# A decoder block on one Trainium2 core: the linear attention's norm weight loaded as 128 written-out rows

## The chip, the cores and the metric

The program runs on one core of one Trainium2 chip. A core has five engines with a queue of instructions each: TensorE (PE, with weight loads shown as PEld), VectorE (DVE), ScalarE (ACT), GpSimd (POOL) and SyncE (SP). SP and POOL issue the DMA transfers of this kernel; 16 DMA engines carry them. The metric is the device time in microseconds, the median of several runs.

## The reference, cut to what matters

One decoder layer on a sequence of 2048 tokens of width 1024: a modulation from a condition vector, a norm, one input projection whose columns go to a gated linear attention (4 heads of 128 values) and to a dilated softmax attention, an output projection, and then a convolution feed-forward network. All in float32. The part that the change touches is the linear attention's output: each head's 128 values are normalised, multiplied by a weight `norm_g` of 128 numbers, the same for all 4 heads, and by a gate.

```python
def rms_norm(x, g):
    xf = x.astype(jnp.float32)
    y = xf * lax.rsqrt(jnp.mean(xf * xf, axis=-1, keepdims=True) + EPS)
    return (y * g.astype(jnp.float32)).astype(x.dtype)
...
    o = o.transpose(1, 0, 3, 2, 4).reshape(B, S, H, GLA_DV)     # H = 4, GLA_DV = 128
    o = rms_norm(o, norm_g).reshape(B, S, H * GLA_DV)
    return (o * jax.nn.silu(r.astype(jnp.float32))).astype(r.dtype)
```

## The kernel before

The tokens are cut into four chunks of 512 (T); every tile has 128 partitions (P) of 512 columns. A matrix product in float32 precision is done as three products of rounded parts: each weight block is loaded into `wraw` (2 buffers), split by ACT into `whi` (L240) and by DVE into `wlo` (L241), each with 4 buffers, and `mm3` issues hi times hi, hi times lo, lo times hi (L306 to L308) into a PSUM tile `psg` (4 buffers). So a weight block passes DMA, ACT, DVE and PE in turn.

`run` first computes the modulation and the first norm. Meanwhile it multiplies the first four weight blocks of the input projection (the tuple FIRST, blocks g0 to g3) with the normalised input tile by tile; their four results stand in all four `psg` buffers. Then it calls `consts`, whose loads wait (through `after`) for one of the last instructions of the modulation. Next comes the projection of chunk 0 in the order of ORDER0: "g0 g1 g2 g3" copy the four results out of PSUM (L523, on ACT, into stage tiles that POOL stores), "V0" is a product with 272 columns (24 matmuls for each of four PSUM tiles, named `psg_516`, `psg_543`, `psg_581` and `psg_608` below), and "W1" is the output gate, where the norm weight comes in (L552). Beside it `stats` loads the tokens of chunk 1 (L1119, tile `sq`, 3 buffers, issued by POOL), squares them on ACT (L426) and adds the squares on DVE (L429, L431).

A scheduler that works with a simulated timeline sets the order of the instructions on each engine, so a changed transfer can also move instructions that the source leaves alone. Engines run their queues in order: an ACT instruction that waits holds all behind it.

The lines that the change touches load and use the norm weight; the weight is a row of 128 numbers in memory, and the tile `gB` holds it four times side by side in every partition:

Of the kernel before, what the change touches and what calls it, by code (L numbers as in the profile page):

```python
# [10 lines left out]
F32 = mybir.dt.float32  # L11
# [3 lines left out]
ALU = mybir.AluOpType  # L15
# [4 lines left out]
P = 128  # L20
# [68 lines left out]
def scale_table():  # L89

    h = 2 * np.arange(4)[None, :] + np.arange(P)[:, None] // 64
    return 0.125 * 2.0 ** (h + 1.0)
# [42 lines left out]
class K:  # L135
# [49 lines left out]
    def consts(self):  # L185
        nc, A = self.nc, self.A
        self.ct = self.const.tile(list(CONSTS.shape), F32, name="consts_sb")
        self.after(nc.sync.dma_start(self.ct, A["consts"]))
        n0 = len(self.loads)
        self.mk = self.cload("masks", MASKS.shape, U32)  # L190
        self.halo = self.const.tile([P, 44, 2], F32, name="halo")

        raw = self.at.tile([P, T], F32, name="graw", tag="pt", bufs=5)
        self.gw = self.const.tile([96, 256], F32R, name="gw")
        self.tie(nc.vector.memset(raw[0:96, 0:256], 0.0), self.lastmm)
        for r in (0, 32, 64):
            self.loads.append(nc.sync.dma_start(raw[r:r + 16, 0:256], A["gla_w_gate"]))
            if r < 64:
                self.loads.append(nc.sync.dma_start(raw[r + 16:r + 17, 0:256], A["gla_b_gate"]))
        nc.vector.tensor_copy(self.gw, raw[0:96, 0:256])  # L200
        nc.vector.tensor_tensor(self.gw[32:64], raw[32:64, 0:256], self.gw[32:64].bitcast(F32), op=ALU.subtract)
        self.gB = self.const.tile([P, 4, P], F32, name="gB")
        g = A["gla_norm_g"]
        self.loads.append(nc.sync.dma_start(self.gB, bass.AP(tensor=g.tensor, offset=g.offset, ap=[[0, P], [0, 4], [1, P]])))
        for ld in self.loads[n0:]:
            self.after(ld)
        self.blk = self.const.tile([P, P], F32R, name="blk")

        self.tie(nc.vector.tensor_copy(self.blk, self.C("blk")), self.lastmm)
        self.tri = self.const.tile([P, P], F32R, name="tri")  # L210
        self.tie(nc.vector.tensor_copy(self.tri, self.C("tri")), self.lastmm)
        self.st = self.const.tile([P, 4, P], F32, name="state")
        nc.vector.memset(self.st, 0.0)
        self.sb = []
        for i in range(2):
            t = self.const.tile([P, 4, P], F32, name=f"sbd{i}")
            nc.vector.memset(t, 0.0)
            self.sb.append(t)
# [254 lines left out]
    def proj(self, c, hs, hook=None, done=()):  # L473
        nc, A, D = self.nc, self.A, self.D[c]
# [3 lines left out]
        def stage(tag=None):  # L478
            if tag:
                return self.up.tile([P, T], F32, name="stg", tag=tag)  # L480
            return self.xp.tile([P, T], F32, name="stg", tag="x")
# [47 lines left out]
        def wide(b):  # L529

            pss = [self.pg() for _ in range(4)]
            for j in range(4):
                w = self.weights("w_tokw", b, j)
                order = [(i, s) for i in range(2) for s in range(4)]
                if j == 3:

                    order.sort(key=lambda x: x[1])
                for i, s in order:
                    h, l = hs[2 * j + i]
                    tk = slice(s * P, (s + 1) * P)  # L540
                    self.mm3(pss[s], [(h[:, tk], l[:, tk])], w[i:i + 1], i == 0 and j == 0, True)
                if j < 3:
                    yield
            for s in range(4):
                off = b and put_off
                st = stage("y0" if off else None)
                if b:
                    r = stage("y1" if off else None)
                    nc.scalar.activation(st, pss[s], AF.Tanh, scale=0.5)
                    nc.scalar.copy(r, pss[s])  # L550
                    nc.vector.scalar_tensor_tensor(st, st, 1.0, r, op0=ALU.add, op1=ALU.mult)
                    nc.vector.scalar_tensor_tensor(st, st, 0.5, self.gB.rearrange("p a b -> p (a b)"), op0=ALU.mult, op1=ALU.mult)  # L552
                else:
                    nc.scalar.copy(st, pss[s])
                self.dq.dma_start(D["rg" if b else "gv"][s * P:(s + 1) * P, :], st)
            if b == 1 and hook:
                hook()
            yield
# [35 lines left out]
        def stores(g):  # L594

            for i, _ in enumerate(g):
                if late and i == 0:
                    next(late.pop(), None)
                yield

        ops = dict(W=wide, V=av, g=glaqk, q=qk)
        order = ORDER if c else ORDER0
        if put_off:
            order = order[:-1]
            self.tail = wide(1)
# [559 lines left out]
def pack_blocks(w, cols):  # L1165

    Kk, N = w.shape
    return w.reshape(Kk // P, P, N // cols, cols).transpose(2, 1, 0, 3).reshape(N // cols, P, (Kk // P) * cols)


def pack_down(w):
    out = []
    for g in range(6):
        n = 4 if g < 5 else 2
        out.append(pack_blocks(w[g * 512:g * 512 + n * P], 1024 // n))
    return np.concatenate(out)


def pack_tok(x):

    return x.T.reshape(KD, P, NCH, T).transpose(2, 0, 1, 3)


def colv(v):
    return v.reshape(-1, P).T


def layout(x, c, w_ada, b_ada, norm1_g, w_in, gla_w_gate, gla_b_gate, gla_norm_g, q_norm_g, k_norm_g, w_out, norm2_g, w_up, conv_w, conv_b, w_down):
    w = w_in[0]
    wide = lambda a: a.reshape(4, 2, P, T).transpose(0, 2, 1, 3).reshape(4, P, 2 * T)  # L1190
    half = lambda a, n: pack_blocks(a, n).reshape(-1, P, 2, 4 * n).transpose(0, 2, 1, 3)
    twice = lambda a: np.concatenate([a, a])[:, None]
    tabs = np.concatenate([colv(norm1_g[0]), colv(norm2_g[0]), colv(b_ada[0]), twice(q_norm_g[0]), twice(k_norm_g[0]), conv_w[0].reshape(3, 44, P).transpose(2, 0, 1).reshape(P, 132), colv(conv_b[0]), scale_table()], 1).astype(np.float32)
    arrs = dict(
        consts=CONSTS, masks=MASKS,
        xT=pack_tok(x[0]), c=c[0], tables=tabs,
        w_ada=w_ada[0].T.reshape(48, P, 1024),
       
        w_av0=half(np.concatenate([w[:, 2576:2832], w[:, 1536:1552]], 1), 272)[0],
        w_av1=half(w[:, 2832:3088], 256)[0],  # L1200
        w_tokw=np.stack([wide(w[:, 512:1024]), wide(w[:, 1024:1536])]),
        w_ch=pack_blocks(np.concatenate([w[:, 0:512], w[:, 1552:2576]], 1), P),
        gla_w_gate=gla_w_gate[0], gla_b_gate=gla_b_gate, gla_norm_g=gla_norm_g,
        w_out=pack_blocks(w_out[0], P), w_up=pack_blocks(w_up[0], P), w_down=pack_down(w_down[0]),
    )
    return {n: np.ascontiguousarray(a) for n, a in arrs.items()}
# [16 lines left out]
```

## Time and profile before

| | |
|---|---|
| median of 3 runs | 2603.27 us (2602.47 to 2603.3) |
| span of the profiled execution | 2603.1 us |
| instructions | 46834 |
| busy: PE, PEld | 98%, 81% |
| busy: DVE, ACT, POOL | 74%, 49%, 17% |
| DMA moved, mean rate | 405.13 MB, 156 GB/s |

The profile is one execution; the runs were timed apart. Times in its rows are microseconds from the start of the span. A row of the timeline reads: start, duration, engine, line, operation, what it writes and reads, its shape, how many in a row, and in brackets how long its engine stood idle before it and what ended that. In a row of a table of waits stand the waiting instruction, what it waited for, the sum, the number and the longest. A row of a stretch reads: the stretch, its length, the busy time of PE, PEld, DVE, ACT and POOL with the number of instructions, the granted clock of TensorE as a share of full speed, the mean busy share of the 16 DMA engines, and GB/s.

### The profile page before, as it was taken

What the parts mean: (1) busy time and instruction counts of PE and PEld (TensorE: products, weight loads), DVE (VectorE), ACT (ScalarE), POOL (GpSimd) and SP (SyncE); (2) the same over time, 40 slices, a digit from 0 to 9 for tenths busy, and PEclk for the clock granted to TensorE, in tenths of its full rate; (3) what the DMA queues carried; (4) which work ended last, traced back from release to release, by engine and by line L of the source; (5) the groups of instructions that cost most, each with busy time, mean ns of one, the idle gap of its engine ahead of it and who ended that gap; (6) DMA issues with size and microseconds to landing.
All of it is one profiled execution on the core that took longest, in us unless ns stands there. A gap on an engine that the chain in (4) does not pass through costs nothing.

```text
span 2603.1 us, 46834 instructions
## 1 busy us (share of the span) xinstructions
PE 2559.7 (98%) x18142; PEld 2104.0 (81%) x18142; DVE 1930.2 (74%) x4091; ACT 1277.7 (49%) x2626; POOL 444.4 (17%) x816
## 2 busy tenths in 40 slices
PE   5999999999999999999999999999999999999999
PEld 4888888788788888887788888878888888788887
DVE  7578877768788777777987777689777775766665
ACT  4566556656454444454545544346445453433332
POOL 1343332313210000012100000310000003100001
PEclk8999999999999999999999999999999999999999
DMA  8766675756633344455334344733443435432322
GB/s 291 242 226 234 211 236 170 239 167 201 230 108 100 123 128 122 127 174 199 123 96 139 117 134 136 252 131 114 129 140 127 143 103 189 150 103 97 96 96 84
DMA packets 164194, 405.13 MB, mean 156 GB/s; under 512 B 19154, under 2 KB 61956, under 8 KB 162692
## 3 DMA queue, kind: packets, MB, share of 16 engines
q0 software_dynamic: 88128, 308.59, 35.5%
q1 hardware_dynamic: 75844, 93.55, 11.6%
q8 instruction: 143, 2.34, 0.4%
q14 instruction: 79, 0.65, 0.1%
HBM read 339.15 MB, written 62.91 MB: 154 GB/s over the span
## 4 chain that ended last, share of the span: by engine, by line
PE 77%; issue 1%; DVE 1%; DMA 1%; ACT 0%; POOL 0%; POOLq 0%; DVEq 0%; ACTq 0%
PE psg L306 22%; PE psg L307 22%; PE psg L308 22%; PE psa L850 2%; PE psa L830 2%; PE psa L954 2%; PE psa L680 1%; PE psa L949 1%; PE psa L865 0%; PE psa L753 0%; PE psa L752 0%; PE psa L969 0%; DMA wada<-in_w_ada_dram 0%; PE psa L757 0%; PE psa L779 0%
## 5 line engine op out<-in xcount | busy, mean ns | idle before, releaser
L306 PE MATMUL psg<-hhi,whi 128*128 128x512 f32 x1992 | 782.0, 396 | 9.2 <-ACT hhi L467 5.3
L307 PE MATMUL psg<-hlo,whi 128*128 128x512 f32 x1992 | 782.9, 394 | 6.7 <-DVE hlo L469 6.5
L308 PE MATMUL psg<-hhi,wlo 128*128 128x512 f32 x1992 | 780.2, 392 | 0.7 <-DVE wlo L241 0.7
L240 ACT CAST whi<-wraw 128x1024 fp32r<-128x1024 f32 (+1 forms) x391 | 410.4, 1051 | 467.4 <-PE psg L307 363.2
L241 DVE TENSOR_TENSOR wlo<-wraw,whi 128x1024 fp32r<-128x1024 f32 (+1 forms) x391 | 478.0, 1223 | 187.2 <-ACT whi L240 181.5
L306 PEld LDWEIGHTS psg<-hhi,whi 128*128 128x128 f32 x1992 | 375.0, 189 | 95.2 <-ACT hhi L467 9.3
L307 PEld LDWEIGHTS psg<-hlo,whi 128*128 128x128 f32 x1992 | 375.3, 188 | 86.7 <-DVE hlo L469 9.6
L308 PEld LDWEIGHTS psg<-hhi,wlo 128*128 128x128 f32 x1992 | 375.5, 188 | 80.6 <-issue 1.7
L306 PE MATMUL psg<-ghi,whi 128*128 128x512 f32 x744 | 295.1, 398 | 0.0
L307 PE MATMUL psg<-glo,whi 128*128 128x512 f32 x744 | 292.1, 393 | 0.5 <-DVE glo L999 0.5
L308 PE MATMUL psg<-ghi,wlo 128*128 128x512 f32 x744 | 291.6, 392 | 0.0
L234 POOL DMA_DIRECT2D wraw<-in_w_up_dram x176 | 93.6, 532 | 982.6 <-DVE wlo L241 850.5
L1073 DVE SCALAR_TENSOR_TENSOR x<-psg,mod,x 128x512 f32<-128x512 f32 x192 | 143.2, 749 | 118.2 <-PE psg L308 115.7
L306 PE MATMUL psg<-whi,hhi 128*128 128x512 f32 (+2 forms) x512 | 172.8, 345 | 8.3 <-ACT stg L523 6.2
L308 PE MATMUL psg<-whi,hlo 128*128 128x512 f32 (+2 forms) x512 | 174.8, 345 | 0.0
L307 PE MATMUL psg<-wlo,hhi 128*128 128x512 f32 (+2 forms) x512 | 174.6, 343 | 0.1
L306 PEld LDWEIGHTS psg<-ghi,whi 128*128 128x128 f32 x744 | 139.5, 188 | 34.0 <-issue 5.3
L307 PEld LDWEIGHTS psg<-glo,whi 128*128 128x128 f32 x744 | 139.8, 188 | 30.0 <-issue 1.9
L308 PEld LDWEIGHTS psg<-ghi,wlo 128*128 128x128 f32 x744 | 139.7, 188 | 29.5 <-issue 0.7
L840 ACT ACTIVATE big<-big,nm 128x256 f32<-128x256 f32 (+1 forms) x256 | 122.4, 480 | 33.6 <-DVE nm L855 33.4
L1028 ACT ACTIVATE y<-psg,tables_sb 128x512 f32<-128x512 f32 x176 | 136.1, 776 | 4.5 <-PE psg L308 3.2
L1029 DVE SCALAR_TENSOR_TENSOR y<-psg,tables_sb,y 128x511 f32<-128x511 f32 x176 | 130.7, 743 | 3.7 <-ACT y L1028 3.6
(253 smaller groups left out, 3621.9 us busy)
## 6 DMA issues: line engine op xcount, KB each, us to landing
wraw<-in_w_up_dram POOLq DMA_DIRECT2D x176, 512.0 KB, 3.6
wraw<-in_w_down_dram POOLq DMA_DIRECT2D x88, 512.0 KB, 3.6
wraw<-in_w_ch_dram POOLq DMA_DIRECT2D x44, 512.0 KB, 4.3
v<-v SPq DMA_DIRECT2D x68, 256.0 KB, 5.6
wada<-in_w_ada_dram POOLq DMA_DIRECT2D x64, 256.0 KB, 4.8
wraw<-in_w_tokw_dram POOLq DMA_DIRECT2D x32, 512.0 KB, 4.2
wraw<-in_w_out_dram POOLq DMA_DIRECT2D x32, 512.0 KB, 4.7
sq<-in_xT_dram POOLq DMA_DIRECT2D x48, 256.0 KB, 4.9
```

The costliest lines, as they stand in the source:

```text
L234: self.dq.dma_start(raw[:, :n], src)
L240: nc.scalar.copy(hi[:, :n], raw[:, :n])
L241: nc.vector.tensor_tensor(lo[:, :n], raw[:, :n], hi[:, :n].bitcast(F32), op=ALU.subtract)
L306: nc.tensor.matmul(ps, wh, hh, start=first and k == 0, stop=False, skip_group_check=shared)
L307: nc.tensor.matmul(ps, wh, hl, start=False, stop=False, skip_group_check=shared)
L308: self.lastmm = nc.tensor.matmul(ps, wl, hh, start=False, stop=k == n - 1, skip_group_check=shared)
L830: nc.tensor.matmul(at(i, hh, z), q[H[hh], i * P:(i + 1) * P], key(H[hh], i, z), start=True, stop=True, skip_group_check=True)
L840: nc.scalar.activation(t[:, lo:hi], t[:, lo:hi], AF.Exp, bias=nm[:, hh, g, i:i + 1], scale=2.0 ** -(h + 1), accum_out=dn[:, hh, g, i:i + 1])
L850: nc.tensor.transpose(ps[:n, i * P:(i + 1) * P], part(S[hh], i), self.C("id"))
L1028: nc.scalar.activation(y, ps, AF.Identity, bias=self.cb[:, b:b + 1], scale=self.cw[:, 2, b:b + 1])
L1029: nc.vector.scalar_tensor_tensor(y[:, 1:], ps[:, :T - 1], self.cw[:, 1, b:b + 1], y[:, 1:], op0=ALU.mult, op1=ALU.add)
L1073: nc.vector.scalar_tensor_tensor(x1, ps, self.mod[:, 40 + cb:41 + cb], x1, op0=ALU.mult, op1=ALU.add)
```

## The change

The host writes the weight out as a 128 x 128 array, the same row 128 times. The load copies that array, one row of 512 bytes to each partition, in place of an access pattern that reads the single row in memory 4 times for each of 128 partitions. The tile is 128 columns wide instead of 512, and the multiplication reads it through a view that repeats the 128 columns for the four heads.

```diff
-        self.gB = self.const.tile([P, 4, P], F32, name="gB")
-        g = A["gla_norm_g"]
-        self.loads.append(nc.sync.dma_start(self.gB, bass.AP(tensor=g.tensor, offset=g.offset, ap=[[0, P], [0, 4], [1, P]])))
+        self.gB = self.cload("gla_norm_g", (P, P))
...
-                    nc.vector.scalar_tensor_tensor(st, st, 0.5, self.gB.rearrange("p a b -> p (a b)"), op0=ALU.mult, op1=ALU.mult)
+                    heads = lambda t: t.rearrange("p (a n) -> p a n", a=4)
+                    nc.vector.scalar_tensor_tensor(heads(st), heads(st), 0.5, self.gB[:, None, :].to_broadcast([P, 4, P]), op0=ALU.mult, op1=ALU.mult)
...
-        gla_w_gate=gla_w_gate[0], gla_b_gate=gla_b_gate, gla_norm_g=gla_norm_g,
+        gla_w_gate=gla_w_gate[0], gla_b_gate=gla_b_gate, gla_norm_g=np.broadcast_to(gla_norm_g.reshape(1, P), (P, P)),
```

`cload` allocates a tile of the given shape and loads the input of that name into it on SP. The new code is shorter, so lines behind it have numbers lower by 2 (by 1 from L552 on). On every engine the number of instructions stays the same. A few change places: around the copies of the first four results and the first narrow product, and again in the stage near 660 to 690 us. On ACT, before, behind the squares of chunk 1's tokens (`sq`), the four copies out of PSUM (`stg` from `psg`) and the casts of weight blocks (`whi`):

```order
L426 ACTIVATE sq_489<-sq_489 128x512
L426 ACTIVATE sq_575<-sq_575 128x512
L240 CAST whi_499<-wraw_497 128x1088
L523 ACTIVATE stg_471<-psg_210 128x512
L523 ACTIVATE stg_474<-psg_211 128x512
L240 CAST whi_505<-wraw_503 128x1024
L523 ACTIVATE stg_481<-psg_212 128x512
L523 ACTIVATE stg_486<-psg_213 128x512
L426 ACTIVATE sq_670<-sq_670 128x512
```

The same place with the change:

```order
L424 ACTIVATE sq_489<-sq_489 128x512
L424 ACTIVATE sq_575<-sq_575 128x512
L238 CAST whi_499<-wraw_497 128x1088
L521 ACTIVATE stg_471<-psg_210 128x512
L238 CAST whi_505<-wraw_503 128x1024
L521 ACTIVATE stg_474<-psg_211 128x512
L521 ACTIVATE stg_481<-psg_212 128x512
L424 ACTIVATE sq_670<-sq_670 128x512
L521 ACTIVATE stg_486<-psg_213 128x512
```

The cast of block `wraw_503` has moved ahead of the second copy, and a square ahead of the fourth. On PE, in the first narrow product, before:

```order
L307 MATMUL psg_516<-wlo_494,hhi_294 128x272
L308 MATMUL psg_516<-whi_493,hlo_296 128x272
L306 MATMUL psg_516<-whi_499,hhi_309 128x272
L306 MATMUL psg_543<-whi_493,hhi_233 128x272
L307 MATMUL psg_543<-wlo_494,hhi_233 128x272
L308 MATMUL psg_543<-whi_493,hlo_235 128x272
```

With the change:

```order
L305 MATMUL psg_516<-wlo_494,hhi_294 128x272
L306 MATMUL psg_516<-whi_493,hlo_296 128x272
L304 MATMUL psg_516<-whi_499,hhi_309 128x272
L305 MATMUL psg_516<-wlo_500,hhi_309 128x272
L306 MATMUL psg_516<-whi_499,hlo_311 128x272
L304 MATMUL psg_516<-whi_499,hhi_320 128x272
```

Before, the second tile `psg_543` begins after 13 matmuls of the first; now all 24 of the first are done ahead of it, and the 14th reads `wlo_500`, which DVE makes of the block that ACT casts first. `psg_543` stands in the buffer that the second copy empties.

## The prediction

> **What bounds the kernel now.** I read the page's busy times first, then the table of waits of PE over the whole run, then the neighbourhood of its longest waits.
>
> ```profile
> PE 2559.7 (98%) x18142; PEld 2104.0 (81%) x18142; DVE 1930.2 (74%) x4091; ACT 1277.7 (49%) x2626; POOL 444.4 (17%) x816
> PE psa L445 <- ACT sq L1092: 11.2, 1, 11.2
> PE psg L307 <- DVE hlo L469: 6.5, 4, 2.4
> PE psg L306 <- ACT stg L523: 6.2, 2, 5.6
> ```
>
> TensorE is the bound: it is busy 98% of 2603.1 us, so only its own idle time, or a slower clock under it, can be won back. One wait of 11.2 us is the start. The second longest single wait, 5.6 us, is for an evacuation at L523. Here is what stood before it, first on PE, then on ACT, then on DVE:
>
> ```profile
> 54.33 0.39 PE L308 MATMUL psg<-hhi,wlo 128*128 128x512 f32 x1
> 55.46 0.39 PE L307 MATMUL psg<-hlo,w 128*128 128x512 f32 x1
> 55.69 0.39 PE L308 MATMUL psg<-hhi,w 128*128 128x512 f32 x1
> 61.72 0.59 PE L306 MATMUL psg<-whi,hhi 128*128 128x272 f32 x1 [5.64 <-ACT stg L523]
> 51.03 0.63 ACT L426 ACTIVATE sq<-sq 128x512 f32<-128x512 f32 x1 [1.13 <-DMA sq<-in_xT_dram]
> 58.89 1.29 ACT L426 ACTIVATE sq<-sq 128x512 f32<-128x512 f32 x2 [7.23 <-DMA sq<-in_xT_dram]
> 60.09 1.08 ACT L240 CAST whi<-wraw 128x1088 fp32r<-128x1088 f32 x1
> 61.08 1.08 ACT L523 ACTIVATE stg<-psg 128x512 f32<-128x512 f32 x2
> 62.87 1.05 ACT L240 CAST whi<-wraw 128x1024 fp32r<-128x1024 f32 x1 [0.72 <-DMA wraw<-in_w_ch_dram]
> 61.20 1.29 DVE L241 TENSOR_TENSOR wlo<-wraw,whi 128x1088 fp32r<-128x1088 f32 x1 [0.16 <-ACT whi L240]
> ```
>
> The copy that PE waits for could have run at 54.72, when the last matmul of the first block ended (54.33 + 0.39). It stands behind two squares on ACT, and these waited 7.23 us for loads of x. Those loads were issued early, from POOL, while SP issued the norm weight:
>
> ```profile
> 46.75 0.43 SPq L204 DMA_DIRECT2D gB<-in_gla_norm_g_dram  x1
> 46.43 0.54 POOL L1119 DMA_DIRECT2D sq<-in_xT_dram  x1 [6.02 <-DVE G L371]
> 46.97 0.54 POOL L383 DMA_DIRECT2D wada<-in_w_ada_dram  x1
> 47.50 1.07 POOL L1119 DMA_DIRECT2D sq<-in_xT_dram  x2
> 48.56 0.54 POOL L383 DMA_DIRECT2D wada<-in_w_ada_dram  x1
> 49.09 0.54 POOL L234 DMA_DIRECT2D wraw<-in_w_ch_dram  x1
> DMA to landing us min/median/max: 11.7/11.7/11.7
> ```
>
> The last row is that of the norm weight alone (tile gB). The DMA queues in three stretches, 49.2 to 50, 51 to 57 and 58 to 60 us, in that order (packets, MB, share of 16 engines; q0 is POOL's queue, q1 SP's), and the rate by stretch:
>
> ```profile
> q0 software_dynamic: 44, 0.18, 54.9%
> q1 hardware_dynamic: 170, 0.14, 51.1%
> ...
> q1 hardware_dynamic: 364, 0.18, 86.0%
> q0 software_dynamic: 61, 0.23, 13.1%
> ...
> q0 software_dynamic: 242, 0.82, 101.5%
> ...
> 51.00:54.00 3.00, 3.00 (x15) 2.49 (x14) 0.43 (x1) 0.63 (x1) 0.54 (x1) 1.00 1.04 44
> 58.00:60.00 2.00, 0.00 (x0) 0.00 (x0) 0.45 (x1) 1.07 (x2) 0.00 (x0) 1.00 1.05 416
> ```
>
> From 51 to 57 the 16 engines are full (86.0 + 13.1%) and move almost nothing: 44 GB/s between 51 and 54. 364 packets of SP's queue, 0.18 MB or about 500 B each, hold them 0.86 x 16 x 6 = 82.6 us, 227 ns apiece. Only the norm weight's packets (512 of 512 B, one row read again and again) have that size there. In 49.2 to 50 the same queue's 170 packets (the masks, mostly) took 0.511 x 16 x 0.8 / 170 = 38 ns each. As soon as the norm weight has landed (46.75 + 11.7 = 58.45), POOL's loads run at 416 GB/s.
>
> **The wait's second cost, the clock.**
>
> ```profile
> 60.98:67.80 6.82, 6.08 (x27) 6.08 (x28) 5.36 (x10) 4.76 (x9) 5.96 (x12) 0.50 0.80 261
> 67.80:74.60 6.80, 6.80 (x56) 6.80 (x56) 2.54 (x5) 2.29 (x7) 2.00 (x3) 1.00 0.96 321
> 511.50:514.90 3.40, 1.81 (x7) 0.99 (x6) 3.40 (x8) 1.86 (x4) 1.87 (x4) 1.00 0.88 299
> 514.90:518.40 3.50, 3.50 (x11) 2.72 (x10) 3.50 (x8) 0.41 (x1) 1.14 (x3) 0.51 0.78 253
> ```
>
> The third number from the end is the granted clock. After the idle stretch it is 0.50 for 6.82 us: 27 matmuls in 6.08 us are 225 ns each, against 6.80 / 56 = 121 ns for the same 272-column form right behind. That is 27 x 0.104 = 2.8 us. The lower two rows show that less is enough: 1.81 us of work in 3.40 was followed by 3.5 us at 0.51.
>
> **The change part by part.** (1) The load. 512 packets of one row become 128 packets of 128 rows, 64 KB. Their price is not in the trace: at 38 ns (the masks) they hold the engines 128 x 0.038 / 16 = 0.3 us, at 227 ns 1.8 us. I take 0.3, since the masks' rows, too, lie one behind another, and keep 1.8. The issue on SP stays one instruction at the same place. (2) What that frees. The square that matters needs POOL's fourth load, so 4 x 0.262 = 1.05 MB, of which 0.18 had moved by 50.0. The other 0.87 MB at 416 GB/s take 2.1 us: landing at 50.0 + 2.1 + 0.3 = 52.4, or 53.9 with the dear packets. From the two squares' start to PE's start the trace has 61.72 - 58.89 = 2.83 us (two squares, a cast, a copy), so ACT would let PE go at 55.2, or 56.7. PE itself is ready at 55.69 plus one step of 0.23 (55.46 to 55.69), 55.92. The wait falls from 61.72 - 55.92 = 5.8 us to 0, at the dear price to 0.8. I book 0.4. Without the idle stretch the clock stays, 2.8 us more. (3) The multiply at L552 reads its weight with a repeated outer step instead of a full row. No row has this form; nearest are
>
> ```profile
> L552 DVE SCALAR_TENSOR_TENSOR stg<-stg,gB x16: 683/686/697, 190.2 to 753.3; 128x512 f32<-128x512 f32 x16
> 659.92 0.69 DVE L934 TENSOR_TENSOR pt<-psa,f 128x512 f32<-128x512 f32 x1
> 664.98 0.46 PE L680 MATMUL psa<-kt 64*32 64x32 f32 x32 [0.64 <-DVE stage L972]
> 666.83 0.50 PE L307 MATMUL psg<-glo,whi 128*128 128x512 f32 x1 [0.50 <-DVE glo L999]
> ```
>
> L934, whose second operand is repeated too, takes 0.69 us. So zero; at the worst twice the time, 11 us on DVE in 16 pieces, which is 74% busy and copies PSUM out ahead of this step on ACT, so PE sees none of it unless the stage buffers run short. (4) Moved instructions. On ACT the cast of the next weight block now stands ahead of the second copy (shown above). PE does all 24 matmuls of its first narrow group before the second group, which needs that copy at 55.92 + 24 x 0.121 = 58.8. The block is POOL's sixth load: 0.79 MB after the fourth, 1.9 us, so it lands at 54.3 (55.8); behind the first copy, which ends near 55.3, the cast (62.87 to 63.83, 0.96 us) and a copy of 0.6 end near 56.9: 1.9 us of cover. PE's 14th matmul now needs DVE's L241 at 55.92 + 13 x 0.121 = 57.5. That step ended 62.49 - 58.89 = 3.6 us after the squares' start, so at 56.0: 1.5 us of cover. Two groups of rows move again near 665 us, where PE waits 0.64 and 0.50 (last rows above): gain or loss up to 1.1, booked at zero. (5) After 68 us PE was idle little, so what is won there is kept only if the other engines move with it. ACT, DVE and POOL stood in the same queue for the same loads, so they do.
>
> Sum: 5.8 + 2.8 - 0.4 = 8.2 us. The profiled span, 2603.1, is 0.2 below the median 2603.27; 2603.3 - 8.2 = 2595.1. No change that a measurement tells is within 0.2%, 5.2 us: 2598.1 to 2608.5.
>
> The Trainium skill, TensorE: Matmul & The Clock Gate, section Part 1: The HAM clock gate, has the clock halve after an idle window of about 3.4 us, on a free-running grid. The trace agrees on the length (3.5 and 6.8 us at half clock), but a window about half busy was enough. By that rule a residual wait under 3.4 us would keep the full clock and the second term whole; by the row it may not.
>
> **The rivals.** *The loads stay slower than I think* (0.17). The page's mean over the run:
>
> ```profile
> DMA packets 164194, 405.13 MB, mean 156 GB/s; under 512 B 19154, under 2 KB 61956, under 8 KB 162692
> ```
>
> At 156 GB/s the fourth load lands at 50.0 + 5.6 + 0.3 = 55.9 and PE starts at 58.7, 2.8 us late; the sixth (0.79 MB, 5.1 us) at 61.0 lets the second copy end near 62.6, a further 1.0 late; and with that much idle the clock drops as before. 8.6 - 3.8 - 2.8 = 2.0 gained: 2601. For it speaks that the stretch is crowded; against it, 416 GB/s right after. It decides from about 250 GB/s down.
>
> *The loads were late for a reason of their own* (0.12): POOL's queue would have been slow without the norm weight. Then the transfer was hidden, as nobody waits for gB before 190 us, and the time stays, 2603. Against it: the rate changes when its packets start and end. The Trainium skill, DMA: Bandwidth & Descriptors, section Queues, rings and completion order, supports it: each DMA engine takes turns between its queues, packet by packet, so that SP's queue should not lock POOL's out. The rows from 51 to 57 (364 packets against 61) do not show equal turns. By that rule 2603, by the rows 2595.
>
> *The moved cast makes PE wait longer* (0.05, slower). If the sixth load landed later than now, the second copy, which no longer goes ahead of its cast, would hold PE. Now that cast starts at 62.87. PE's 25th narrow matmul came near 61.72 + 24 x 0.225 = 67.1, so loss begins when the cast starts after 67.1 - 0.96 - 0.6 = 65.5, and reaches 5.2 us at 70.7: 2609. For that the load must be 8 us later than with the crowding; only a reordered queue would do it.
>
> **How the numbers follow.** The forecast, wait and slow clock gone, has 0.66: 2595.1, by itself 2591.9 to 2598.3: 0.4 for the residual wait, 1.1 for the rows near 665 us and 1.7 (half of 3.4 us) for a clock drop like that at 514.9, which a shift of 8 us may add or spare, each either way. The range reaches into the slow-loads case, 2601.5: 0.83 inside. Faster takes 0.66 and a little of the 0.17: 0.69. Same: the rest of it and the 0.12, 0.26. Slower 0.05.
>
> **What would show it.** The norm weight lands in about 4 us instead of 11.7; DMA between 51 and 54 moves over 300 GB/s instead of 44; the two squares start near 53 instead of 58.89; PE's first narrow matmul has no wait behind L521 and the granted clock in 60.98 to 67.80 is 1.00. L551 stays near 0.69. I am wrong if the rate at 51 to 54 stays low with the norm weight landed, or if the wait reappears at the second copy.

## The result, and the profile after

With the norm weight written out for 128 partitions the kernel takes 2595.13 us (median of 8 runs, 2592.43 to 2597.49); the kernel before took 2603.2 beside it (8 runs, 2601.48 to 2605.54). The ratio is 0.9968, its 95% interval 0.9959 to 0.9978, so 8.07 us are gained. The profiled execution of after took 2592.85 us with a span of 2591.1 us and lies at the low end of its runs; why is taken up below.

First the busy times on the page of after, and the longest entries in its table of waits of PE (a wait behind L521, which was L523 before, has no row any more):

```profile
PE 2552.5 (99%) x18142; PEld 2099.2 (81%) x18142; DVE 1930.3 (74%) x4091; ACT 1276.8 (49%) x2626; POOL 443.5 (17%) x816
PE psa L443 <- ACT sq L1091: 10.9, 1, 10.9
PE psg L305 <- DVE hlo L467: 6.2, 4, 2.9
...
PE psg L304 <- ACT stg L548: 2.1, 2, 1.5
```

PE is busy 7.2 us less than before for the same 18142 matmuls: most of that is time at half clock which is gone, some 2.7 us here, and nearly 3 us by chance at two places further on (see the end of the section on the prediction). The timeline of after around the place, PE first, then ACT:

```profile
55.41 0.39 PE L306 MATMUL psg<-hhi,w 128*128 128x512 f32 x1
55.90 0.39 PE L304 MATMUL psg<-whi,hhi 128*128 128x272 f32 x1
50.58 0.63 ACT L424 ACTIVATE sq<-sq 128x512 f32<-128x512 f32 x1 [0.98 <-DMA sq<-in_xT_dram]
52.96 1.31 ACT L424 ACTIVATE sq<-sq 128x512 f32<-128x512 f32 x2 [1.75 <-DMA sq<-in_xT_dram]
54.25 1.11 ACT L238 CAST whi<-wraw 128x1088 fp32r<-128x1088 f32 x1
55.26 0.58 ACT L521 ACTIVATE stg<-psg 128x512 f32<-128x512 f32 x1
56.25 1.05 ACT L238 CAST whi<-wraw 128x1024 fp32r<-128x1024 f32 x1 [0.40 <-DMA wraw<-in_w_ch_dram]
57.20 1.08 ACT L521 ACTIVATE stg<-psg 128x512 f32<-128x512 f32 x2
```

The first narrow matmul (second row) has no bracket, yet PE did lose a little. Matmuls that wait for nothing start 0.23 us apart here, so PE was ready at 55.41 + 0.23 = 55.64; the copy ended at 55.26 + 0.58 = 55.84, and PE started at 55.90. That leaves a delay of 0.26 us where before had 61.72 - 55.92 = 5.80. (A bracket counts from the end of the matmul before, which is 0.16 us behind that ready time, so it is 0.16 us shorter than the delay.) The two squares start at 52.96 in place of 58.89.

The norm weight's load and its multiplication in after, then two stretches of the timeline, and POOL's queue from 51 to 57 us:

```profile
DMA to landing us min/median/max: 4.3/4.3/4.3
L551 DVE SCALAR_TENSOR_TENSOR stg<-stg,gla_norm_g_sb x16: 684/694/703, 181.7 to 742.4; 128x512 f32<-128x512 f32 x16
...
51.00:54.00 3.00, 3.00 (x15) 2.49 (x14) 0.80 (x2) 1.21 (x3) 0.54 (x1) 1.00 1.02 404
60.98:67.80 6.82, 6.82 (x56) 6.82 (x56) 2.95 (x6) 2.84 (x7) 2.38 (x4) 1.00 1.04 399
...
q0 software_dynamic: 546, 1.84, 81.1%
```

Where POOL's queue moved 61 packets before, it moves 546; the rate between 51 and 54 us is 404 GB/s in place of 44. In 60.98 to 67.80 there are 56 matmuls at a clock of 1.00 where 27 ran at 0.50.

How much of this is kept shows a wait that both kernels have about 120 us later, behind the same copy (before, then after):

```profile
182.65 0.50 PE L306 MATMUL psg<-whi,hhi 128*128 128x512 f32 x1 [0.64 <-ACT stg L550]
```

```profile
174.15 0.50 PE L304 MATMUL psg<-whi,hhi 128*128 128x512 f32 x1 [0.64 <-ACT stg L548]
```

The place comes 8.50 us earlier: 61.72 - 55.90 = 5.82 up to the first narrow matmul, and 2.68 behind it, from the clock. Of the 5.82, the wait is 5.80 - 0.26 = 5.54. The other 0.28 was there ahead of the load: in this execution the last wide matmul starts at 55.41 instead of 55.69, and SP issues the norm weight at 46.45 instead of 46.75. I use this row as a ruler in every run below, because it has both terms in it and, beside such a shift of the start, little else.

### The profile page after: what moved, and what is told of

The parts are those of the page before. It is cut to its first block, busy times and chain, and to the rows that moved or that the text cites. A ratio compares the mean times of both kernels' runs of the same rounds, so it can differ in the third digit from the quotient of the medians.

```text
span 2591.1 us, 46836 instructions
## 1 busy us (share of the span) xinstructions
PE 2552.5 (99%) x18142; PEld 2099.2 (81%) x18142; DVE 1930.3 (74%) x4091; ACT 1276.8 (49%) x2626; POOL 443.5 (17%) x816
## 4 chain that ended last, share of the span: by engine, by line
PE 78%; issue 1%; DVE 1%; DMA 0%; ACT 0%; POOL 0%; POOLq 0%; DVEq 0%; ACTq 0%
PE psg L304 22%; PE psg L305 22%; PE psg L306 22%; PE psa L849 2%; PE psa L829 2%; PE psa L953 2%; PE psa L679 1%; PE psa L948 1%; PE psa L864 0%; PE psa L752 0%; PE psa L751 0%; PE psa L968 0%; PE psa L756 0%; PE psa L778 0%; DVE sq L463 0%
```

## The experiments

Four theories were tested. A: the many reads of one row held POOL's loads up. B: it was the number of packets, 512 against 128. C: it was the instructions that moved. D: it was the multiplication. Two more kernels ask whether the place of the load matters and whether the clock is a term of its own, and one repeats the edit elsewhere. The kernel before, run beside them, had medians of 2604.26 us (18 runs) in the series of rows4, row128, hot4 and late, and 2603.15 us (28 runs) in that of hot2, warm, mul and cond; each ratio is against the runs of its own series, and across series the ratios are to be compared, not the medians.

**rows4: as many packets as before, each from a row of its own.**

```diff
-        self.gB = self.cload("gla_norm_g", (P, P))
+        self.gB = self.const.tile([P, 4, P], F32, name="gB")
+        self.loads.append(nc.sync.dma_start(self.gB, A["gla_norm_g"].rearrange("a p n -> p a n")))
...
-        gla_norm_g=np.broadcast_to(gla_norm_g.reshape(1, P), (P, P)),
+        gla_norm_g=np.broadcast_to(gla_norm_g.reshape(1, 1, P), (4, P, P)),
```

> As many packets as before, but no shared row: the host writes the weight out 4 x 128 times, and 512 packets of 512 B read 512 different rows into the wide tile. The order of the instructions is that of before on every engine. Theory A (the shared row makes the packets slow): 38 ns a packet, 512 x 0.038 / 16 = 1.2 us on the 16 engines; the fourth load lands near 53.4, ACT lets PE go near 56.2, wait about 0.3, clock stays: 2595 to 2597. Theory B (the number of 512 B packets is what costs): about 227 ns a packet as before, 2603. Theory C (the moved cast and matmuls brought the gain): the order is that of before, so 2603, with fast packets.

Measured: 2595.63 us (5 runs, 2594.01 to 2597.12), ratio 0.9964 (0.9951 to 0.9976). The landing of the load, PE's first narrow matmul, a stretch, and the queues from 51 to 57 us in rows4:

```profile
DMA to landing us min/median/max: 5.4/5.4/5.4
56.88 0.40 PE L305 MATMUL psg<-whi,hhi 128*128 128x272 f32 x1 [0.50 <-ACT stg L522]
51.00:54.00 3.00, 3.00 (x15) 2.49 (x14) 0.43 (x1) 0.63 (x1) 0.54 (x1) 1.00 1.01 342
...
q0 software_dynamic: 545, 1.85, 85.7%
q1 hardware_dynamic: 153, 0.07, 4.0%
```

The 256 KB land in 5.4 us instead of 11.7, and POOL's queue moves as much as in after. B falls. The instructions of rows4 stand in the order of before on every engine, so C falls with it: the gain needs no moved instruction.

**row128: the narrow tile, but 128 reads of one row.**

```diff
-        self.gB = self.cload("gla_norm_g", (P, P))
+        self.gB = self.const.tile([P, P], F32, name="gB")
+        g = A["gla_norm_g"]
+        self.loads.append(nc.sync.dma_start(self.gB, bass.AP(tensor=g.tensor, offset=g.offset, ap=[[0, P], [1, P]])))
```

> The narrow tile of the change, but loaded from the one row in memory, read 128 times; the order of the instructions is that of the changed kernel. Theory A: 128 packets at up to 227 ns, 1.8 us on the 16 engines in place of 0.3; the fourth load about 1.5 us later than in the changed kernel, PE waits 1 to 1.5 us, the clock mostly stays: 2596 to 2598, packets near 200 ns. Theory B: as the changed kernel, 2595, packets near 40 ns. Theory C: 2595.

Measured: 2596.94 us (8 runs, 2594.28 to 2599.13), ratio 0.9971 (0.9961 to 0.9982). The same two rows in row128:

```profile
DMA to landing us min/median/max: 7.4/7.4/7.4
57.26 0.39 PE L306 MATMUL psg<-whi,hhi 128*128 128x272 f32 x1 [1.55 <-ACT stg L523]
```

The order of its instructions is that of after. A quarter of the reads leaves 1.55 us of the wait, and the load lands 3.1 us later than the 128 written-out rows of after (4.3; in cond, below, they took 5.6). One thing was not as expected: the load's packets show 75 ns each (50 packets of SP's queue from 51 to 57 us at 3.9% of 16 engines), not near 200. In time row128 and after cannot be told apart, as their two ratios lie well within each other's intervals; the traces are 175.51 - 174.15 = 1.36 us apart on the ruler.

**hot4 and hot2: after, and beside it the reads of one row.** The kernel after, plus a load that reads one row 512 times (hot4) or 256 times (hot2) into a tile that nobody reads.

```diff
         self.gB = self.cload("gla_norm_g", (P, P))
+        hot = self.const.tile([P, 4, P], F32, name="hot")      # hot2: [P, 2, P]
+        g = A["gla_norm_g"]
+        self.loads.append(nc.sync.dma_start(hot, bass.AP(tensor=g.tensor, offset=g.offset, ap=[[0, P], [0, 4], [1, P]])))
```

> The changed kernel, and behind its own load of the weight the old load once more (one row read 512 times) into a tile that nothing uses. Multiplication and written-out weight stay as changed. Theory A: the wait and the slow clock come back, 8 us: 2602 to 2604, with 44 GB/s between 51 and 54 us. Theory C and any theory that puts the gain into the multiplication or the narrow tile: 2595.

> As the run that added the old load to the changed kernel, with half of its packets (the row read 256 times). Theory A with what the first runs showed (128 reads: squares at 54.4; 512 reads: 57.6 and 58.9): squares near 55.5, PE waits 2 to 2.5 us: 2597 to 2599.5, between the changed kernel (2595) and the full added load (2601). A theory of a fixed cost per load from a shared row: 2601.

Measured: hot4 2601.2 us (11 runs, 2598.2 to 2603.58), ratio 0.9986 (0.9977 to 0.9995), and hot2 2598.91 us (11 runs, 2597.05 to 2600.76), ratio 0.9982 (0.9973 to 0.9991). In hot4 the landing of that load, the two squares, PE's first narrow matmul, three stretches, and the queues from 51 to 57 us:

```profile
DMA to landing us min/median/max: 11.9/11.9/11.9
57.59 1.25 ACT L427 ACTIVATE sq<-sq 128x512 f32<-128x512 f32 x2 [5.06 <-DMA sq<-in_xT_dram]
60.38 0.39 PE L307 MATMUL psg<-whi,hhi 128*128 128x272 f32 x1 [3.64 <-ACT stg L524]
55.24:58.65 3.41, 1.49 (x7) 0.91 (x5) 0.40 (x1) 1.06 (x2) 0.00 (x0) 1.00 0.90 330
58.65:62.06 3.41, 1.68 (x13) 1.69 (x14) 3.04 (x6) 3.41 (x6) 2.51 (x5) 1.00 0.55 195
62.06:65.47 3.41, 3.41 (x29) 3.41 (x29) 3.00 (x4) 2.48 (x6) 3.41 (x8) 1.00 0.76 236
...
q0 software_dynamic: 292, 0.98, 46.0%
q1 hardware_dynamic: 511, 0.25, 14.5%
```

A wait at the same place is back, by a transfer whose data nobody uses. With rows4, where the packets stay and only the shared row goes, this shows A: the reads of one row hold the loads of x up. But hot4 did not do all that was expected. Its median is short of 2602 to 2604, the rate between 51 and 54 us is 203 GB/s and not 44, and POOL's queue moved 292 packets from 51 to 57, between the 61 of before and the 546 of after. The clock stayed at 1.00 through a wait of 3.64 us, so the profiled execution (2598.51 us) paid the wait alone. The other ten runs had mean clocks of 0.994 to 0.996 against its 0.997, which would fit a drop in many of them; none of them has a profile, so that is not shown. PE's wait grows with the number of reads, 1.55 us at 128 (row128), 2.27 at 256 (hot2) and 3.64 at 512 (hot4), and hot2's 2598.91 is not the 2601 of a fixed cost per load; in the ratios of the three, 0.9971, 0.9982 and 0.9986, the intervals overlap. The scheduler placed the copies and the second cast differently in hot4 and hot2 than in after, but the first copy, on which PE waits, stands ahead of all that in each of them.

**late: the load of before, held back until the first block is multiplied.**

```diff
-        self.loads.append(nc.sync.dma_start(self.gB, bass.AP(tensor=g.tensor, offset=g.offset, ap=[[0, P], [0, 4], [1, P]])))
+        self.tie(nc.sync.dma_start(self.gB, bass.AP(tensor=g.tensor, offset=g.offset, ap=[[0, P], [0, 4], [1, P]])), self.lastmm)
```

> The kernel before, with its load of one row 512 times held back until the last matmul of the first four blocks (near 56 us), so that the loads of x for the squares pass ahead of it. The cast of the second block stands ahead of the second copy, as in the changed kernel. Theory A: the load still takes 6 to 8 us of full DMA engines, but at 57 to 65 us, where the next weight blocks have some 5 us of cover; PE's wait of 5.6 us is gone: 2595 to 2598. If the cover is too small, a wait of some us appears at the next block, 2598 to 2602. Theory D (the bytes and engine time of the load cost, wherever it stands): 2603.

Measured: 2594.76 us (5 runs, 2593.86 to 2597.12), ratio 0.9963 (0.9951 to 0.9976). In late the load's issue and landing, PE's first narrow matmul, the stretch behind it, the queues in that stretch, and a cast:

```profile
56.27 0.38 SPq L204 DMA_DIRECT2D gB<-in_gla_norm_g_dram  x1
DMA to landing us min/median/max: 10.1/10.1/10.1
56.34 0.40 PE L306 MATMUL psg<-whi,hhi 128*128 128x272 f32 x1
57.50:61.00 3.50, 3.50 (x30) 3.50 (x30) 2.61 (x4) 3.50 (x9) 2.42 (x5) 1.00 0.28 75
q1 hardware_dynamic: 302, 0.15, 20.2%
q0 software_dynamic: 43, 0.11, 7.7%
...
67.70 1.05 ACT L240 CAST whi<-wraw 128x1024 fp32r<-128x1024 f32 x1 [6.55 <-DMA wraw<-in_w_ch_dram]
```

The same expensive load, 10 us later, costs nothing that the runs' times show. It still holds POOL's queue up (43 packets in 3.5 us, 75 GB/s), and a cast on ACT waits 6.55 us for its weight block, but PE is busy 3.50 of 3.50 us: it has a narrow product's work in front of it. Theory D in the form of this run's forecast, that the load's bytes cost wherever it stands, falls. The trace shows a small remainder: from the first narrow matmul to the ruler late takes 0.73 us longer than after. So the load was dear because of what stood behind it at 47 us.

**warm: before, with PE kept busy in the gap.** 28 more matmuls into a PSUM tile that nobody reads, ahead of the first narrow product.

```diff
+        keep = self.pa()
+        for i in range(28):
+            self.nc.tensor.matmul(keep, ws[3][7][0], h0[7][0], start=i == 0, stop=i == 27)
         self.consts()
```

> The kernel before with 28 more matmuls of 512 columns on PE, whose results nobody reads: 5 of them in the idle stretch near 47 us, 23 behind the last matmul of the first four blocks (23 x 0.227 = 5.2 us), so that PE works through most of the wait for L523. The old load of the weight stays. Theory A (idle time and, apart from it, the slow clock behind it): the first narrow matmul starts at about 61.7 as before, but the granted clock from 61 to 68 us is 1.00, which saves 2.8 us: 2600.5 to 2601.5. If the slow clock were not a matter of the idle stretch, 2604 or, by the added work, more.

Measured: 2600.9 us (11 runs, 2599.89 to 2605.34), ratio 0.9993 (0.9984 to 1.0002), which in time alone decides nothing. In warm the added matmuls, PE's first narrow matmul, the stretch behind it, and the ruler:

```profile
56.77 5.38 PE L1116 MATMUL psa<-hhi,w 128*128 128x512 f32 x23
61.98 0.28 PE L306 MATMUL psg<-whi,hhi 128*128 128x272 f32 x1
60.98:67.80 6.82, 6.82 (x53) 6.62 (x52) 4.87 (x9) 4.22 (x8) 5.57 (x11) 1.00 0.80 260
180.15 0.50 PE L306 MATMUL psg<-whi,hhi 128*128 128x512 f32 x1 [0.64 <-ACT stg L550]
```

None of the 28 ran near 47 us, as was expected of five: all start between 53.8 and 61.8 us, five among the last wide matmuls and 23 behind them. The narrow product starts 0.26 us later than before (61.98 against 61.72), held by the added work alone (it follows the last added matmul at the usual step, the copy being long done at 61.1), with the loads about as late as before (the two squares start at 58.35), and yet the ruler comes 182.65 - 180.15 = 2.50 us earlier. So the clock is a term of its own, 2.50 + 0.26 = 2.76 us in these two traces.

**mul: before's load, the multiplication with a repeated operand.**

```diff
-                    nc.vector.scalar_tensor_tensor(st, st, 0.5, self.gB.rearrange("p a b -> p (a b)"), op0=ALU.mult, op1=ALU.mult)
+                    nc.vector.scalar_tensor_tensor(st.rearrange("p (a n) -> p a n", a=4), st.rearrange("p (a n) -> p a n", a=4), 0.5, self.gB[:, 0:1, :].to_broadcast([P, 4, P]), op0=ALU.mult, op1=ALU.mult)
```

> The other half of the change alone: the old load of one row 512 times, and the multiplication reading the first 128 columns through a repeated step. The order of the instructions is that of before on every engine. Theory A: as before, 2603 to 2605, L552 at 0.68 to 0.70 us. If the repeated operand brought or cost anything, 2595 or over 2606.

Measured: 2603.38 us (11 runs, 2602.0 to 2605.58), ratio 0.9999 (0.9991 to 1.0008). The multiplication and PE's wait in mul:

```profile
L552 DVE SCALAR_TENSOR_TENSOR stg<-stg,gB x16: 679/694/702, 189.4 to 752.8; 128x512 f32<-128x512 f32 x16
60.95 0.60 PE L306 MATMUL psg<-whi,hhi 128*128 128x272 f32 x1 [5.20 <-ACT stg L523]
```

The multiplication takes 694 ns here and 686 in before; over all runs the same operation lies between 678 (row128, repeated operand) and 694, so 8 ns cannot be laid to the operand. The wait is there as before. D, the multiplication, falls.

**cond: after, with the condition vector written out as well.** At the program's start SP loads the 4 KB condition vector into every partition, one row read 128 times; here the host writes out 128 rows.

```diff
-        nc.sync.dma_start(self.cond, bass.AP(tensor=c.tensor, offset=c.offset, ap=[[0, P], [1, 1024]]))
+        nc.sync.dma_start(self.cond, c)
...
-        xT=pack_tok(x[0]), c=c[0], tables=tabs,
+        xT=pack_tok(x[0]), c=np.broadcast_to(c[0].reshape(1, 1024), (P, 1024)), tables=tabs,
```

> The changed kernel with the other load from a shared row written out too: the condition vector, 4 KB, read 128 times at the very start, becomes 128 rows. Order as in the changed kernel. Theory A: the same sort of load, but 128 reads of 4 KB, which landed in 4.1 us; at most 0.6 us earlier: 2594.5 to 2595.5, which the runs can hardly tell from the changed kernel. If shared rows cost per byte, a gain of 2 us or more: under 2593.5.

Measured: 2595.38 us (6 runs, 2594.26 to 2596.21), ratio 0.9968 (0.9956 to 0.998), the same as after. The first use of the vector, and the step behind it, in cond:

```profile
4.08 1.06 ACT L325 ACTIVATE big<-cond 128x1024 f32<-128x1024 f32 x1 [2.05 <-DMA cond<-in_c_dram]
6.15 0.63 ACT L424 ACTIVATE sq<-x 128x512 f32<-128x512 f32 x1 [1.00 <-DMA x<-in_xT_dram]
```

The vector lands 1 us earlier (3.3 us against 4.3 in after, where its first use starts at 5.13), but the next step waits for x, and starts at 6.15 (6.09 in after). A cost for each byte of a shared row, which would have given under 2593.5, is not seen. Reading a row of 4 KB 128 times costs about 1 us here, and it is hidden.

The runs side by side; the last column is the start of the ruler's row:

| run | reads of one row | landing | two squares start | PE waits | first narrow matmul | clock 60.98 to 67.80 | ruler | median |
|---|---|---|---|---|---|---|---|---|
| before | 512 | 11.7 | 58.89 | 5.64 | 61.72 | 0.50 | 182.65 | 2603.2 |
| mul | 512 | 10.3 | 58.11 | 5.20 | 60.95 | 0.56 | 181.88 | 2603.38 |
| hot4 | 512 | 11.9 | 57.59 | 3.64 | 60.38 | 1.00 | 178.64 | 2601.2 |
| hot2 | 256 | 8.7 | 55.58 | 2.27 | 59.04 | 1.00 | 177.66 | 2598.91 |
| row128 | 128 | 7.4 | 54.44 | 1.55 | 57.26 | 1.00 | 175.51 | 2596.94 |
| rows4 | 0 (512 rows) | 5.4 | 54.03 | 0.50 | 56.88 | 1.00 | 175.14 | 2595.63 |
| after | 0 (128 rows) | 4.3 | 52.96 | 0.10 | 55.90 | 1.00 | 174.15 | 2595.13 |
| late | 512, later | 10.1 | 52.83 | 0.10 | 56.34 | 1.00 | 175.32 | 2594.76 |

PE's wait is counted from the end of the matmul before. In hot2 and hot4 the landing is that of the added load; in hot2 the two squares run apart, the second at 56.88. From after to hot4 the ruler moves 178.64 - 174.15 = 4.49 and the first narrow matmul 60.38 - 55.90 = 4.48: what the first narrow matmul is late, the ruler is late. Not all of that is the load's: hot4's last wide matmul starts at 56.34, 0.93 us behind that of after, so the wait accounts for 3.64 - 0.10 = 3.54. Before and mul, with the low clock, have 2.68 us more on the ruler than at the first narrow matmul; late has 0.73 and hot2 0.37 more, and the other runs nothing.

None of the variants is shown to be faster than after: late, cond and rows4 agree with it within their intervals.

## Why the prediction was right

**The sum.** 8.2 us were forecast, 8.07 measured; the interval of the ratio stands for 5.7 to 10.7 us, so an agreement to 0.1 us is luck in part. The wait: 5.8 less a residual of 0.4 was forecast, 5.80 less 0.26 is in the traces. The clock: 2.8 forecast, 2.68 by the ruler and 2.76 by warm. Both terms are thus right in kind and in size.

**What the norm weight held up.** The landing is 4.3 us where I said about 4, and the rate is 404 GB/s where I said over 300. The squares start at 52.96: near 53, as the list of signs has it, but the sum itself had the load landed at 52.4 and ACT done at 55.2. ACT was done at 55.84, and the 0.7 us that it was to have in hand before PE's 55.92 were not there. That PE starts at 55.90, where I had 55.92, is a coincidence: PE was ready 0.28 us earlier than in before, and then waited 0.26.

**The unknown price of the new load.** Of 38 and 227 ns a packet I took the lower. The load did come out cheap, but the reason was too simple: 227 ns is not a price that such a packet has. Mul, which keeps the load of before at its place, shows 230 ns from 51 to 57 us (330 packets at 79.0%). But in hot4 the 511 packets of SP's queue took 0.145 x 16 x 6 / 511 = 27 ns each, and in late 302 took 0.202 x 16 x 3.5 / 302 = 37 ns, and both loads landed about as late and held POOL's queue up, though in hot4 less than in before. I had read "the engines are full" from 86.0 + 13.1%; in late the same load holds POOL's queue up with the engines 28% busy. What is alike is the pace: 330 packets of SP's queue in 6 us in mul, 364 in before, 511 in hot4, and 302 in 3.5 us in late, 55 to 86 a microsecond. The step of the prediction that says what holds the loads up (the packets' time on the engines) is thus not the mechanism, at least in late, though the effect that it was used for is there; what the mechanism is stays open.

**The moved instructions.** The cast moved ahead of the second copy was to end, with that copy, near 56.9; the copies run from 57.20, so the first of them ends near 57.7 (half of the 1.08), under the 58.8 at which PE needs it. The cover was 1.1 us rather than 1.9, and it held. The weight block behind that cast landed at 48.79 + 7.4 = 56.2, where I had 54.3. DVE's step for PE's 14th matmul ended at 55.39 + 1.29 = 56.7 instead of 56.0, still ahead of 57.5. Near 665 us PE's waits of 0.64 and 0.50 became 0.64 and 0.51, as booked.

**The multiplication.** 694 ns against 686, where 690 was forecast.

**The rivals.** Slow loads (2601): against it stands 404 GB/s. Loads late for a reason of their own (2603): rows4 and hot4 rule it out. The rule it drew on stands in the Trainium skill, DMA: Bandwidth & Descriptors, section Queues, rings and completion order: an engine goes round its queues packet by packet, and a packet there is a bundle of typically 9 to 17 descriptors. The prediction set the trace's counts, 364 packets of SP's queue to 61 of POOL's, against it. No row here shows whether a packet of the trace is such a bundle, and the packets differ in size: in bytes the two queues moved 0.18 and 0.23 MB in before and 0.15 and 0.11 MB in late. So these counts neither bear the rule out nor contradict it, and equal turns alone would not have meant 2603: a queue whose turns are long holds up the one that it takes turns with. The moved cast (2609): the wait did not reappear.

**A coincidence to keep out of the gain.** The profiled spans differ by 2603.1 - 2591.1 = 12.0 us, which is more than the 8.07 of the medians. The same waits further on show where the rest is, in before and then in after:

```profile
513.59 0.49 PE L306 MATMUL psg<-whi,hhi 128*128 128x512 f32 x1 [1.49 <-ACT stg L550]
2237.18 0.47 PE L306 MATMUL psg<-hhi,whi 128*128 128x512 f32 x1 [1.46 <-ACT hhi L467]
```

```profile
504.44 0.50 PE L304 MATMUL psg<-whi,hhi 128*128 128x512 f32 x1 [1.48 <-ACT stg L548]
2226.55 0.47 PE L304 MATMUL psg<-hhi,whi 128*128 128x512 f32 x1 [1.47 <-ACT hhi L465]
```

9.15 us at the first, 10.63 at the second, 12.0 at the end. Behind both waits before has a stretch at half clock and after has none; they account for 10.63 - 9.15 = 1.48 and 12.0 - 10.63 = 1.37 us of it, while the 0.65 us between the ruler and the first of these waits is not explained. The stretches of each wait and of what follows the second, before and then after:

```profile
2235.30:2238.70 3.40, 1.84 (x7) 0.96 (x6) 3.40 (x6) 2.77 (x4) 0.59 (x2) 1.00 0.76 292
2238.70:2242.10 3.40, 3.40 (x10) 2.61 (x9) 3.40 (x6) 0.72 (x1) 0.82 (x2) 0.50 0.36 131
```

```profile
502.00:505.40 3.40, 1.82 (x8) 0.97 (x7) 3.40 (x7) 2.19 (x5) 1.75 (x4) 1.00 0.85 300
505.40:508.80 3.40, 3.40 (x17) 2.82 (x16) 3.40 (x8) 0.00 (x0) 1.48 (x3) 1.00 0.76 278
...
2224.60:2228.00 3.40, 1.84 (x8) 0.95 (x7) 3.40 (x6) 2.84 (x4) 0.55 (x1) 1.00 0.78 283
2228.00:2231.40 3.40, 3.40 (x17) 2.74 (x15) 3.40 (x5) 0.73 (x1) 0.80 (x2) 1.00 0.36 134
```

The same wait of about 1.5 us, the same 1.84 us of work in 3.40, and once the clock halves for 3.4 us and once it does not. I had allowed 1.7 us either way for one such drop; the profiled pair happens to differ by two. That this is chance and not the change shows in the other traces: behind 70 us there are two such stretches in before, mul, warm, rows4, hot2 and late, one in row128 and cond, and none in hot4 and after, whether the load reads one row or not. A run's time is 1.7 to 1.8 us above its span (2592.85 and 2591.1 in after), so the profiled execution of before stands for about 2604.9 us, an estimate. That is 1.7 above its median, and after's is 2.3 below its own: together the 4 us by which the spans differ more than the medians. (The prediction set the span 2603.1 beside the median 2603.27 as if they were the same measure; its sum starts from the median and is not touched.)

## What to carry to other kernels

A load that broadcasts by reading one short row hundreds of times is small in bytes, but it can hold up the loads of another queue for as long as it runs; look at what is in flight beside it, and write the rows out or issue it where the bound engine has work in front of it. A table of waits does not name such a load: nobody waited for the norm weight, and the wait that it caused showed three steps later, at a copy out of PSUM. To separate such a gain from chance, follow one late wait that both kernels have: its shift, less what the two executions already differ by ahead of the change, is the gain of the place, and what is added behind it is something else.

## What the runs showed of the hardware

Reads of one row run at a pace of their own. 512 reads of one 512-byte row landed after 11.7, 11.9, 10.3 and 10.1 us (before, hot4, mul, late), 256 after 8.7 (hot2), 128 after 7.4 (row128); 512 reads of different rows landed after 5.4 (rows4), and 128 after 4.3 and 5.6 (after, cond). A row of 4 KB read 128 times cost only about 1 us of landing (4.3 us in after, 3.3 written out, in cond).

The recorded time of such packets is no measure of it: 227 ns in before, 230 in mul, 75 in row128, 27 in hot4, 37 in late. Why they differ stays open. In hot4 the row is the first of a 64 KB array, in before it is all of a 512-byte one, but late reads that same 512-byte array, so the array alone does not set the packets' time. It also stays open why hot4 let POOL's queue move 292 packets from 51 to 57 us where before let 61; mul, with the load of before, let 133.

The clock is not decided by the idle share of a stretch laid around one wait alone. The Trainium skill, TensorE: Matmul & The Clock Gate, section Part 1: The HAM clock gate, ties the drop to an idle window of about 3.4 us on a free-running grid. The length of the slow stretches agrees, 3.4 to 3.5 us after the short waits; but hot4's 3.64 us of waiting were followed by no drop, and 1.84 us of work in 3.40 once by a drop and once by none, so a stretch that was only in part idle was enough. A free grid would let the same gap fall differently in two executions, but no row here shows the grid.
